# Weight sums of a split product moved from the attention stage to the up product, with a new order in the linear attention

## The chip, the cores and the metric

The kernel runs on one core of one Trainium2 chip. The metric is device time of one execution, in microseconds (us); the median of the runs shown is used. The engines are TensorE (PE: matmuls and transposes, into PSUM), VectorE (DVE), ScalarE (ACT), GpSimd (POOL) and SyncE (SP). SP issues most loads and stores on the hardware queue q1; POOL issues the transfers that add into memory, and others, on the software queue q0. Both queues are carried by the same 16 DMA engines.

## The reference

One layer of a streaming encoder, on 1024 prompt and 32 sample tokens (1056 columns in all), model width 1024:

```python
h = rms_norm(x, g_pre_mix)
qa, ka, va, ra, alr, qb, kb, vb, ga, gb = split_cols(h @ w_in)
oa, s_gla = gla_branch(qa, ka, va, ra, alr, w_a2, b_a2, g_gla, gla_s0, gla_block)
ob, k_rows, v_rows = attn_fn(qb, kb, vb, rel_bias)
mix = (jax.nn.sigmoid(ga) * (oa @ w_br_a) + jax.nn.sigmoid(gb) * (ob @ w_br_b)) @ w_out
x = x + rms_norm(mix, g_post_mix)
f, conv_new = conv_ffn(rms_norm(x, g_pre_ffn), conv_s0, w_up, conv_w, conv_b, w_down)
x = x + rms_norm(f, g_post_ffn)
gate = jax.nn.sigmoid(rms_norm(x, g_pre_ple) @ w_ple_gate)
x = x + rms_norm(gate * (pe @ w_ple), g_post_ple)
```

`gla_branch` is a gated linear attention (4 heads, blocks of tokens with a carried state), `attn_fn` a softmax attention over a band of 64-frame chunks (8 heads), `conv_ffn` an up product of 2 x 2816 columns, a causal convolution of width 3, gelu, and the down product. All is float32; outputs are the new x, the newest band rows, the states of the linear attention and of the convolution.

## The kernel before

Every matrix product is made from split operands: a float32 value is written as a high part and the remainder, and PE makes three products of the parts (high by high, high by low, low by high). The large products save a further eighth by the Strassen-Winograd scheme: an operand is cut into four quarters, sums of quarters are formed, and seven products of sums replace eight. So besides its own weights a product needs *sums of weight quarters*.

The program is one long function, `emit`, with stages one after the other: the per-layer embedding product; the input projection (`in_strassen`); the band attention; the linear attention; the branch products; the out product; the up product (`up_strassen`, 22 blocks f); the down product (28 units of seven by four); the last gate.

**Weight sums.** For the down product they lie in the DRAM tensor `d_ws` (4 sums of 4 parts, 704 KB each), for the branch product in `d_wa` (16 parts of 256 KB). POOL makes each by three DMAs: a one-element write into the target from a tile that has just been computed (`at`; it sets the earliest time), a copy of the first quarter from DRAM to DRAM, and an accumulating copy of the second quarter. The accumulation is put off: `second_sum` keeps a list `later` and issues the oldest entry when more than two are waiting. The down product loads `d_ws[1]` for its fifth unit first.

**Band attention.** For each of four head pairs, two heads: nine steps (j = 0 to 8) of scores, exponentials, transposes and value products; a head is a group g. Engine orders of PE, DVE and ACT follow the program text here; POOL's and SP's are set by a planner. The loop makes one part of a weight sum of `d_wa` at j = 1, 4, 7 and of `d_ws` at j = 2, 5, 8, from the second group on, until there are 16. In the last group the first gate decays of the linear attention are begun (`decays(0)`): POOL loads `d_alr` into a tile that the scores of the group before have used, and the next step's matmul (L1188) reads it. `band_end` turns the sums of the exponentials into reciprocals and stores them to `d_inv` from a tile of tag `ot` (two buffers), which the evacuations L1055 use too.

**Filler.** PE's gaps in both attention stages are filled with pieces of the rest of the input projection: `piece` emits some 9 to 12 matmuls; `fill["n"]` counts pieces. Their PSUM tiles are evacuated by functions kept in `fill["done"]`, called by `flush` (all) or `tidy` (all but the newest). The first 117 pieces belong to plain tiles of three pieces a unit, the next 112 are whole units (`MAIN` = 229). The band runs up to 120 pieces, the preamble of the linear attention up to 126 (`GLA_FIRST`).

**Linear attention.** 16 units u (4 heads by 4 segments). In each: products of the levels into PSUM, score copies by DVE, a transpose of scores (`score_turn`, with ACT's copy into `turned`), the column copy `score_last` by DVE into `turned` (L1453), factors, exponentials and differences for unit u + 1, results of unit u - 1, the outputs (L1521) which read `turned`, the next unit's start, and the inverse roots (`roots`). Nine calls of `slot` a unit may each emit one piece; a condition paces them.

**Up product.** Block f computes one tile of a and one of g. `q` is the single tile of tag `c22` that holds a partial sum (L2586); `av` has three buffers; `sm` (L2367) is a single tile of quarter sums, stored by POOL (L2364). Blocks in `AHEAD` have two of their products made earlier and take 5, not 7. In this loop the planner orders all engines.

Of the kernel before, what the change touches and what calls it, by code (L numbers as in the profile page):

```python
# [114 lines left out]
def emit(tc, a):  # L115
# [118 lines left out]
    def log_exp():  # L234
        tc.keep_in_program_order(ac.preload_act_table_set("natural_log_exp_and_others"))
# [664 lines left out]
    def piece():  # L900
        if fill["now"] is None:
            if fill["at"] == len(units):
                return
            fill["now"] = unit_parts(*units[fill["at"]]), 0
        tidy()
        lows()
        parts, n = fill["now"]
        next(parts)
        i, c = units[fill["at"]]
        item = isinstance(tiles[i], Item)  # L910
        fill["now"] = (parts, n + 1) if n < 2 and not item else None
        if n == 0 and fill["split"] == i + 1 <= FIRST and (c in (0, 2) if item else c < 2):
            split_half(int(c > 0))
            if c:
                fill["lows"].append(load_tile)
        if fill["now"] is None:
            fill["at"] += 1
        fill["n"] += 1
        if fill["n"] in PLACES:
            place(*PLACES[fill["n"]])  # L920

    def flush():
        for f in fill["done"]:
            f()
        fill["done"].clear()
# [226 lines left out]
    def weight_sum(i, m, at):  # L1152
        x, y = WSUMS[i]
        po.dma_start(d_ws[i, m, 0:1, 0:1], at)
        po.dma_start(d_ws[i, m], x[m])
        second_sum(d_ws[i, m], y[m])
# [100 lines left out]
    for i in range(len(WORK) + SK + 1):  # L1257
        g, j = divmod(i, NW)
        hp, hd = divmod(g, 2)
        if g < 8:  # L1260
            if j == 0:
                if hd == 0:
                    band_sums(hp)
                steps = prepare(g + 1) if g < 7 else decays(0)
            if j == 3 and hd == 0:
                B[hp]["ob"] = evt()
            WORK[i][0]()
            if SK <= i:
                WORK[i - SK][1]()
            B[hp]["exp"].pop()()  # L1270
            next(steps, None)
            if j % 3 == 2:
                next(made, None)
            if j % 3 == 2 and g:
                n = 3 * (g - 1) + j // 3
                if n < 16:
                    weight_sum(*divmod(n, 4), B[hp]["sums"][hd][0:1, 0:1])
            if hd == 0 and hp < 3 and j in (5, 7) or hd and hp < 3 and j == 0:
                band_row(hp + 1, {5: 0, 7: 1, 0: 2}[j])
            if g == 7 and j in (6, 7):  # L1280
                head_value(0, j - 6)
            if j % 3 == 1 and g:
                n = 3 * (g - 1) + j // 3
                if n < 4 * HK:
                    branch_sum(n, B[hp]["sums"][hd][0:1, 0:1])
        piece()
        n = i - SK - 1
        if n >= 0 and WORK[n][2]:
            WORK[n][2]()
        if len(WORK) <= i < len(WORK) + SK:  # L1290
            WORK[i - SK][1]()
        for f in LOWS:
            f()
        LOWS.clear()
        flush()
        if fill["n"] < 18 + (BAND_PIECES - 18) * (i + 1) / (len(WORK) + SK + 1):
            piece()
        next(end, None)
        if n >= 0 and n % (2 * NW) == 2 * NW - 1:
            end = band_end(n // (2 * NW))  # L1300
            next(end)
    flush()
    while fill["now"]:
        piece()
        flush()
    next(end)
    while later:
        second_sum()
# [41 lines left out]
    def differences(u, ls):  # L1350
        g, h, s, t0, nt = seg(u)
        b = g["b"]
        if ls[0] == 1:
            X[u] = tl(gp, [P, 8, 288], tag="x", bufs=2)
        x = X[u]
        for l in ls:
            m, w = 1 << l, level_width(l, nt)
            bv = b[:, 0, t0 : t0 + w]
            at, ref = [bass.AP(bv.tensor, bv.offset + o, [bv.ap[0], [2 * m, w // (2 * m)], [T + e, 2], [d, m]]) for o, e, d in ((0, m, 1), (m - 1, 0, 0))]
            ve.tensor_tensor(x[:, l - 1, :w].rearrange("p (n h m) -> p n h m", h=2, m=m), at, ref, op=ALU.subtract)  # L1360
# [91 lines left out]
    def score_last(u):  # L1452
        ve.copy_predicated(turned.rearrange("p (n s) -> p n s", s=2)[:, :, 1], masks[:, 0, 1], R[u]["dg"][:, 0:64])  # L1453
# [198 lines left out]

    slots = [0]

    def slot(k=1):
        for i in range(k):
            slots[0] += 1
            if OB.get("h") is not None or fill["n"] < min(MAIN, GLA_FIRST + (MAIN - GLA_FIRST) * slots[0] / (9 * 14.7)):
                piece()

    level_start(0)
    for u in range(16):
        h, s = divmod(u, 4)
        if s == 0:
            if h == 3:
                rows_times = branch_rows()
                next(rows_times, None)
            if h < 3:
                if h:
                    head(h + 1)  # L1670
                chain = decays(h + 1)
        flush()
        loads(u)
        if u < 15:
            differences(u + 1, range(1, 5))
        if s == 3:
            next(chain, None)

        def states():
            if u < 15:  # L1680
                slot(2)
                key_copies(u)
            if u:
                output_copies(u - 1)
            if u == 15:
                gate_sigmoid(0)
                gate_sigmoid(1)
            if s == 3:
                next(chain, None)
            updates(u)  # L1690

        def turn_back():
            if u == 15:
                slot(2)
            if u:
                output_turns(u - 1)
            slot(1)

        level_products(u, (states, turn_back))
        flush()  # L1700
        if u < 15:
            exponentials(u + 1, (1, 2, 3, 4))
            flush()
        score_copies(u, range(4, 7))
        slot(1)
        score_turn(u)
        if u < 15:
            exponentials(u + 1, (7, 6))
        if u:
            results(u - 1)  # L1710
        if u == 15:
            gates(u)
            gate_sigmoid(2)
            gate_sigmoid(3)
            branch_split(1)
        if u < 15:
            differences(u + 1, (5,))
        score_last(u)
        if u < 15:
            factors(u + 1, (7, 1, 2))  # L1720
        flush()
        slot(1)
        if s == 3:
            next(chain, None)
        if u < 15:
            factors(u + 1, (3, 4, 6))
            exponentials(u + 1, (5,))
        tidy()
        slot()
        flush()  # L1730
        if s < 2 and h:
            turn_values(h, 2 + 4 * s)
        outputs(u)
        if u < 15:
            level_start(u + 1)
        squares_a(u)
        if u < 15:
            factors(u + 1, (5,))
        else:
            branch_split(2)  # L1740
        if u >= 12:
            next(rows_times, None)
        flush()
        n = (5, 4, 2, 0)[s]
        steps_of(lambda: next(chain, None), n - n // 2)
        tidy()
        slot()
        if s < 2 and h:
            turn_values(h, 4 + 4 * s)
        flush()  # L1750
        steps_of(lambda: next(chain, None), n // 2)
        slot()
        if s == 2 and h < 3:
            head_value(h + 1, 0)
            head_value(h + 1, 1)
        if u == 14:
            while fill["n"] < MAIN:
                piece()
                flush()
            xp.release()  # L1760
            key_copies(15)
            eb = pool("eb", side="right")
            bo = pool("bo", side="right")
            for x in "hl":
                OB[x] = tl(bo, [P, 4, T], F32R, tag="b" + x)
            branch_split(0)
            split_tile()
            load_tile()
            gate_rows(1)
        if u == 15:  # L1770
            log_exp()
        roots(u)
        flush()
        if u < 15:
            gates(u)
        if u < 14:
            slot()
        if u == 13:
            next(rows_times, None)
            gate_rows(0)  # L1780
# [713 lines left out]
    def up_strassen(f):  # L2494
# [89 lines left out]
        Z_ = Z[:, :, :HC]  # L2584
        mul(Z, weight(s1, WL_ENG[2]), "t1", True, True)
        ve.tensor_tensor(q, p1, Z_, op=ALU.add)  # L2586
        if not ahead:
            mul(X, weight(a12, WL_ENG[3]), "b21", False, True)
            ac.activation(c11, X_, AF.Copy)
# [704 lines left out]
```

## Time and profile before

| | us |
|---|---|
| median of 3 runs | 1894.21 (1894.15 to 1895.33) |
| profiled execution, its own time | 1898.3 |
| its span, first to last instruction | 1896.4 |
| PE busy in it | 1831.3 |
| granted TensorE clock, mean | 0.988 |

A row of the busy table gives an engine's busy time and its count of instructions. A row of a stretch gives its bounds and length, then the busy time and count for PE, PEld (weight loads), DVE, ACT and POOL, the granted TensorE clock, the busy share of the DMA engines and the GB/s. In a timeline row the first two numbers are start and duration; the bracket at the end is the idle time just before it on that engine, and what ended it. A row of DMA issues gives how many, the KB of one, and the median time from issue to landing. A queue's row gives packets, MB and the share of the 16 engines' time. "waits" rows say who waited for what: total, times, longest.

### The profile page before, as it was taken

How to read it: one execution, taken by the hardware profiler on the slowest of the kernel's cores; microseconds unless marked ns; L12 is line 12 of the kernel's file. 1: busy time of each engine (PE TensorE's matmuls, PEld its weight loads, DVE VectorE, ACT ScalarE, POOL GpSimd, SP SyncE). 2: the span in 40 equal slices, each digit the busy share in tenths (PEclk: the TensorE clock that was granted, in tenths of full speed). 3: DMA queues.
4: the chain of work that ended last, by engine and by line, in shares of the span. 5: the costliest groups of instructions: out<-in, count | busy, mean ns of one | idle time of the engine just before them, and what ended most of it. 6: DMA issues, size and time to landing. Idle time of an engine off the chain costs nothing.

```text
span 1896.4 us, 36233 instructions
## 1 busy us (share of the span) xinstructions
PE 1831.3 (97%) x14000; PEld 1791.7 (94%) x14000; DVE 1301.3 (69%) x2451; ACT 1005.1 (53%) x2126; POOL 369.0 (19%) x641
## 2 busy tenths in 40 slices
PE   8999999999959999999999999999999999999996
PEld 8999998999958999898999999999999999999996
DVE  6955543666625777677856775888888875558776
ACT  7544233666626776766646455433333345555555
POOL 0043431243311222110000111111122210000112
PEclk9999999999979999999999999999999999999998
DMA  7288987799985889976777377455557679887746
GB/s 283 81 232 236 277 205 219 213 257 301 263 199 183 247 240 258 243 172 199 274 221 226 111 267 286 154 196 166 181 168 184 168 202 297 281 292 240 237 150 109
DMA packets 169402, 413.24 MB, mean 218 GB/s; under 512 B 21957, under 2 KB 56973, under 8 KB 168333
## 3 DMA queue, kind: packets, MB, share of 16 engines
q1 hardware_dynamic: 111548, 244.34, 39.5%
q0 software_dynamic: 56240, 161.90, 33.0%
q10 hardware_dynamic: 1440, 4.69, 0.6%
q8 instruction: 110, 1.80, 0.4%
q14 instruction: 64, 0.52, 0.1%
HBM read 270.68 MB, written 181.97 MB: 239 GB/s over the span
## 4 chain that ended last, share of the span: by engine, by line
PE 56%; DVE 4%; ACT 4%; DMA 3%; issue 1%; SPq 1%; DVEq 0%; ACTq 0%; POOLq 0%
PE two L2523 6%; PE two L2521 6%; PE two L2522 6%; PE mm L228 3%; PE mm L226 3%; PE mm L227 3%; PE two L2968 3%; PE two L2966 3%; PE two L2967 3%; PE mm L859 2%; PE mm L860 2%; PE mm L861 2%; PE two L2430 1%; PE two L2432 1%; PE two L2431 1%
## 5 line engine op out<-in xcount | busy, mean ns | idle before, releaser
L2968 PE MATMUL two<-d,wlo 128*128 128x264 f32 x616 | 174.4, 283 | 1.0 <-DVE wlo L2702 1.0
L2967 PE MATMUL two<-d,whi 128*128 128x264 f32 x616 | 174.7, 284 | 0.2 <-DVE d L2653 0.2
L2966 PE MATMUL two<-d,whi 128*128 128x264 f32 x616 | 174.6, 284 | 0.0
L2511 ACT ACTIVATE whi<-ws 128x512 fp32r<-128x512 f32 x88 | 55.5, 632 | 161.5 <-PE two L2522 159.6
L859 PE MATMUL mm<-xh,whi 128*128 128x264 f32 x448 | 134.8, 301 | 3.7 <-ACT fv L867 3.6
L860 PE MATMUL mm<-xl,whi 128*128 128x264 f32 x448 | 127.4, 284 | 0.0
L861 PE MATMUL mm<-xh,wlo 128*128 128x264 f32 x448 | 127.2, 284 | 0.0
L2522 PE MATMUL two<-ml,whi 128*128 128x264 f32 x448 | 126.4, 283 | 0.0
L2523 PE MATMUL two<-mh,wlo 128*128 128x264 f32 x448 | 126.0, 284 | 0.0
L2521 PE MATMUL two<-mh,whi 128*128 128x264 f32 x448 | 125.8, 284 | 0.0
L2968 PEld LDWEIGHTS two<-d,wlo 128*128 128x128 f32 x616 | 116.4, 189 | 1.5 <-DVE wlo L2702 1.5
L2967 PEld LDWEIGHTS two<-d,whi 128*128 128x128 f32 x616 | 115.8, 188 | 0.4 <-DVE d L2653 0.4
L2966 PEld LDWEIGHTS two<-d,whi 128*128 128x128 f32 x616 | 115.7, 188 | 0.0
L890 PE MATMUL mm<-xh,whi 128*128 128x352 f32 x312 | 111.0, 356 | 2.0 <-ACT fv L734 2.0
L892 PE MATMUL mm<-xh,wlo 128*128 128x352 f32 x312 | 103.0, 330 | 0.0
L891 PE MATMUL mm<-xl,whi 128*128 128x352 f32 x312 | 102.8, 330 | 0.0
L642 PE MATMUL two<-tl,whi 128*128 128x264 f32 x320 | 90.7, 284 | 0.0
L641 PE MATMUL two<-th,whi 128*128 128x264 f32 x320 | 90.7, 283 | 0.0
L643 PE MATMUL two<-th,wlo 128*128 128x264 f32 x320 | 90.7, 284 | 0.0
L859 PEld LDWEIGHTS mm<-xh,whi 128*128 128x128 f32 x448 | 84.9, 190 | 5.6 <-ACT fv L867 5.0
L2702 DVE TENSOR_TENSOR wlo<-wraw,whi 128x512 fp32r<-128x512 f32 (+1 forms) x81 | 51.8, 644 | 50.1 <-ACT whi L2701 50.0
L860 PEld LDWEIGHTS mm<-xl,whi 128*128 128x128 f32 x448 | 84.5, 189 | 0.0
(801 smaller groups left out, 6876.7 us busy)
## 6 DMA issues: line engine op xcount, KB each, us to landing
raw<-in_w_in SPq DMA_DIRECT2D x36, 512.0 KB, 6.1
d_b<-av POOLq DMA_DIRECT2D x33, 528.0 KB, 3.3
d_ws<-in_w_down POOLq DMA_DIRECT2D x24, 704.0 KB, 15.0
uraw<-d_b SPq DMA_DIRECT2D x32, 528.0 KB, 5.7
raw<-in_w_up SPq DMA_DIRECT2D x29, 512.0 KB, 4.4
d_gs<-in_w_in POOLq DMA_DIRECT2D x48, 256.0 KB, 5.8
sraw<-in_w_up SPq DMA_DIRECT2D x22, 512.0 KB, 3.6
wraw<-d_ws SPq DMA_DIRECT2D x16, 704.0 KB, 5.8
```

The source lines that it names most:

```text
L859: pe.matmul(ps, h[:, k], xh[:, b, s], start=(k == 0 and not (half and x.chain)), stop=False, skip_group_check=True)
L860: pe.matmul(ps, h[:, k], xl[:, b, s], start=False, stop=False, skip_group_check=True)
L861: pe.matmul(ps, l[:, k], xh[:, b, s], start=False, stop=(k == HK - 1), skip_group_check=True)
L890: pe.matmul(ps, wh, h[:, k, s], start=(k == 0), stop=False)
L891: pe.matmul(ps, wh, l[:, k, s], start=False, stop=False)
L892: pe.matmul(ps, wl, h[:, k, s], start=False, stop=(k == cnt - 1))
L2521: pe.matmul(ps[:, j, :HC], w[0][:, k], x[0][:, k, s], start=st, stop=False, skip_group_check=True)
L2522: pe.matmul(ps[:, j, :HC], w[0][:, k], x[1][:, k, s], start=False, stop=False, skip_group_check=True)
L2523: pe.matmul(ps[:, j, :HC], w[1][:, k], x[0][:, k, s], start=False, stop=sp_, skip_group_check=True)
L2966: pe.matmul(o, wh, xh_[:, s], start=(k == 0 and p in (0, 4, 5)), stop=False, skip_group_check=True)
L2967: pe.matmul(o, wh, xl_[:, s], start=False, stop=False, skip_group_check=True)
L2968: pe.matmul(o, wl, xh_[:, s], start=False, stop=(k == HD - 1 and p in (3, 4, 6)), skip_group_check=True)
```

## The change

The 16 sums of `d_ws` are no longer made in the band; block f of the up product makes part f (for f below 16), held back by its tile `q`, and blocks 16 and 17 issue the last two accumulations. At the band's end exactly one more piece runs, where the kernel before ran pieces until the current unit was done. In the linear attention the pacing of the pieces becomes a fixed pattern: of nine slots the fifth and eighth are left out. The column copy `score_last` goes ahead of the results of unit u - 1 and of the splits and sigmoids of the last unit, and behind the differences of level 5 and the factors of levels 1 and 2, which now come earlier; one `flush` is added between the exponentials of levels 7 and 6; the factors of level 7 come last. In unit 14 the roots are made before the branch operands are split.

```diff
-            if j % 3 == 2 and g:
-                n = 3 * (g - 1) + j // 3
-                if n < 16:
-                    weight_sum(*divmod(n, 4), B[hp]["sums"][hd][0:1, 0:1])
...
     flush()
-    while fill["now"]:
-        piece()
-        flush()
+    piece()
+    flush()
     next(end)
...
+    SKIP = (5, 8)
+
     def slot(k=1):
         for i in range(k):
             slots[0] += 1
-            if OB.get("h") is not None or fill["n"] < min(MAIN, GLA_FIRST + (MAIN - GLA_FIRST) * slots[0] / (9 * 14.7)):
+            if OB.get("h") is not None or fill["n"] < MAIN and slots[0] % 9 not in SKIP:
                 piece()
...
         score_turn(u)
         if u < 15:
-            exponentials(u + 1, (7, 6))
+            exponentials(u + 1, (7,))
+            flush()
+            exponentials(u + 1, (6,))
+            differences(u + 1, (5,))
+            factors(u + 1, (1, 2))
+        score_last(u)
         if u:
             results(u - 1)
...
         if u < 15:
-            differences(u + 1, (5,))
-        score_last(u)
-        if u < 15:
-            factors(u + 1, (7, 1, 2))
+            factors(u + 1, (7,))
         flush()
...
+        if u == 15:
+            log_exp()
+        roots(u)
+        if u == 14:
             branch_split(0)
             split_tile()
             load_tile()
             gate_rows(1)
-        if u == 15:
-            log_exp()
-        roots(u)
...
         ve.tensor_tensor(q, p1, Z_, op=ALU.add)
+        if f < 16:
+            weight_sum(*divmod(f, 4), q[0:1, 0, 0:1])
+        elif f < 18:
+            second_sum()
```

## The prediction

> **What bounds the kernel now.** I read the page's busy table first, then the stretches by stage, then the waits of TensorE, and only then the timeline around the longest of them.
>
> ```profile
> PE 1831.3 (97%) x14000; PEld 1791.7 (94%) x14000; DVE 1301.3 (69%) x2451; ACT 1005.1 (53%) x2126; POOL 369.0 (19%) x641
> ```
> ```profile
> 340.00:520.00 180.00, 177.22 (x1239) 170.00 (x1238) 113.08 (x282) 119.60 (x290) 61.29 (x123) 1.00 0.95 259
> 520.00:545.00 25.00, 19.45 (x127) 18.35 (x126) 10.20 (x24) 10.34 (x27) 3.28 (x8) 0.86 1.03 252
> 545.00:565.00 20.00, 5.29 (x26) 5.02 (x25) 1.14 (x5) 2.26 (x6) 3.53 (x6) 0.66 0.67 158
> 600.00:890.00 290.00, 281.15 (x2060) 261.86 (x2059) 215.94 (x615) 212.78 (x718) 62.44 (x91) 0.99 0.85 235
> 1205.00:1560.00 355.00, 355.00 (x2928) 355.00 (x2927) 300.53 (x489) 136.13 (x183) 69.80 (x132) 1.00 0.61 176
> ```
>
> TensorE (PE, the first busy column) bounds the program: it idles 65 us of 1896.4. So an edit is worth the idle time and lost clock of PE that it removes. The rows are, from the top, the band attention (two parts), its end, the linear attention and the up product. The up product has no idle PE to win, but the last two columns show DMA engines only 61% busy; the band runs them at 95 to 103%. The linear attention idles 8.9 us. The remarkable place is 520 to 565: PE works 24.7 us out of 45.
>
> ```profile
> 523.40 0.82 POOL L1138 DMA_DIRECT2D d_wa<-sums  x1
> 544.71 0.56 POOL L1139 DMA_DIRECT2D d_wa<-in_w_br_a  x1 [19.59 <-DMA d_wa<-sums]
> 549.77 0.83 POOL L1132 DMA_DIRECT2D d_wa<-in_w_br_a  x1 [4.01 <-DMA d_wa<-in_w_br_a]
> 551.27 0.84 POOL L1132 DMA_DIRECT2D d_ws<-in_w_down  x1 [0.66 <-DMA d_ws<-d_ws]
> 551.80 0.86 POOL L1183 DMA_DIRECT2D qs<-d_alr  x1
> ```
> ```profile
> 514.48 0.30 SPq L1175 DMA_DIRECT2D d_inv<-ot  x1
> ...
> 536.64 0.38 ACT L1055 ACTIVATE ot<-one 64x256 f32<-64x256 f32 x1 [6.65 <-DMA d_inv<-ot]
> ...
> 531.55 0.29 PE L1036 MATMUL two<-kl,qs 128*32 128x272 f32 x1
> 538.76 0.47 PE L1035 MATMUL two<-kh,qs 128*128 128x128 f32 x1 [5.30 <-DVE sm L1041]
> 561.76 0.63 PE L1188 MATMUL one<-qs,wa 80*128 80x352 f32 x1 [14.71 <-DMA qs<-d_alr]
> ```
>
> There are two stalls. **The 5.30 us stall:** ACT's evacuation L1055 needs the tile that the 9 KB store of the reciprocal sums still reads, and that store, issued at 514.48, held ACT until 536.64; DVE waits for ACT, PE for DVE. **The 14.71 us stall:** the gate matmul L1188 needs d_alr, whose load POOL issued only at 551.80, because POOL stood 19.59 us on a one-element write and then queued the last sums ahead of the load. Both are DMA delays, and the traffic is on record:
>
> ```profile
> qs<-d_alr POOLq DMA_DIRECT2D x1, 330.0 KB, 9.8
> ```
> ```profile
> q0 software_dynamic: 8032, 30.48, 64.5%
> ...
> d_ws<-in_w_down POOLq DMA_DIRECT2D x23, 704.0 KB, 15.1
> d_wa<-in_w_br_a POOLq DMA_DIRECT2D x24, 256.0 KB, 13.1
> ```
> ```profile
> L1154 POOL DMA_DIRECT2D d_ws<-sums x16: 497/511/817, 351.2 to 523.9; - x16
> ...
> DMA to landing us min/median/max: 4.5/7.5/8.6
> ```
>
> (DMA issues, first from 520 to 562, then queues and issues from 351 to 551, then from the answers on the tiles d_ws and d_inv, with ns min/median/max and first and last start.) POOL's queue q0 takes two thirds of what the engines have. Over the 200 us its 30.48 MB cost 129 us of all 16 engines, 4.23 us a MB. The d_ws sums are 16 copies and 16 accumulations of 704 KB (0.721 MB), so 98 us; the same 32 of 256 KB for d_wa (36 us) stay.
>
> **A. Weight sums leave the band.** 98 us of engine time leave some 200 us (351 to 551), so the busy share falls from about 0.95 to about 0.5. POOL loses 48 issues, the 16 one-element writes with their landing waits among them. The d_inv store then meets half the traffic: ACT wanted its tile at 529.99 (536.64 - 6.65), 15.5 us after the issue, and the other transfers of d_inv land in 4.5 to 8.6 us. I take 5.30 us as gone; at the 22 us of this one it would stay.
>
> ```profile
> d_b<-av POOLq DMA_DIRECT2D x33, 528.0 KB, 3.3
> ```
>
> For the d_alr load the cover is the PE work between the last reader of the old tile (531.55) and L1188: 1.6 us to the first stall (533.46), then 8.3 us to 547.05, of which 2.8 is half clock; 7.1 us. Its need is 0.86 issue plus a landing between 3.3 us (POOL's larger store above) and 9.8 (this one, behind two accumulations): 4.2 to 10.7, so 0 to 3.6 us stay. Nearest is the lower end, since one accumulation of 256 KB at most is ahead; I keep 1.0.
>
> The clock goes with the stalls:
>
> ```profile
> 535.00:540.00 5.00, 0.99 (x5) 0.81 (x6) 2.83 (x8) 2.44 (x6) 0.00 (x0) 0.76 1.08 255
> 540.00:545.00 5.00, 5.00 (x26) 4.91 (x25) 0.00 (x0) 0.84 (x4) 0.29 (x1) 0.56 1.02 332
> ...
> 560.00:565.00 5.00, 3.24 (x12) 3.20 (x12) 0.00 (x0) 1.00 (x2) 0.00 (x0) 0.50 0.26 54
> 565.00:570.00 5.00, 5.00 (x23) 4.71 (x24) 2.08 (x7) 3.17 (x9) 0.00 (x0) 0.67 0.10 36
> ```
>
> Half clock covers 1.2 + 4.4 us of PE work after the first stall and 3.2 + 3.3 after the second; half of that, 2.8 and 3.3 us, is lost. The Trainium skill (TensorE: Matmul & The Clock Gate, What's actually happening) says that an idle window of some 3.4 us halves the clock and a busy one restores it. The trace agrees that the clock halves after both stalls, but it stays half longer than one such window; by the rule alone each stall would cost 1.7 us of clock, 3.4 in place of 6.1, and the forecast would be 2.7 us later.
>
> A gives 5.3 + 14.7 + 2.8 + 3.3 - 1.0 = **25.1 us**.
>
> **B. The same sums in the up product.** Per block f = 0 to 15: a one-element write after the sum L2586, a copy, and the accumulation of two blocks earlier; POOL issues 0.5 + 0.5 + 0.8 us and has 285 idle us there. PE, DVE and ACT get no instruction. The copy waits on POOL for the landing of the one-element write, as the gate sums of the input projection do:
>
> ```profile
> d_gs<-c POOLq DMA_DIRECT2D x32, 0.0 KB, 3.8
> ```
>
> Behind it stand POOL's memsets of gx, which it issues ahead, and the stores of av and sm, for which DVE waits only when their tiles come round. The DMA engines get 98 us over 18 of 22 blocks (0.82 of 355 us, 290), so 0.61 becomes 0.95. What is late then? Two tiles are tight (timeline, DMA issues, timeline):
>
> ```profile
> 1228.10 0.70 DVE L2367 TENSOR_TENSOR sm<-av 128x528 f32<-128x528 f32 x1
> 1241.90 0.70 DVE L2367 TENSOR_TENSOR sm<-av 128x528 f32<-128x528 f32 x1
> ...
> 1229.10 0.77 POOL L2364 DMA_DIRECT2D d_b<-sm  x1 [0.25 <-DVE sm L2367]
> ```
> ```profile
> d_b<-sm POOLq DMA_DIRECT2D x11, 792.0 KB, 6.8
> ...
> sraw<-in_w_up SPq DMA_DIRECT2D x22, 512.0 KB, 3.6
> ```
> ```profile
> 1429.11 0.33 SPq L2497 DMA_DIRECT2D sraw<-in_w_up  x1
> ...
> 1436.57 0.69 DVE L2504 TENSOR_TENSOR ws<-sraw 128x512 f32<-128x512 f32 x1
> ```
>
> The tile sm is single and written every 13.8 us; its store is issued by 1229.87 and lands 6.8 us later, 8.6 us after the write began, so 5.2 us are spare. A copy and an accumulation ahead of it in q0 cost 98 / 16 = 6.1 us: 0.9 us late, and DVE, busy 300.5 of 355 us, has 2.1 spare per 13.8. The second weight tile has 7.5 us from issue to use and lands in 3.6. So cost is between nothing and the rivals below; as TensorE runs with several products of split weights in hand, I take **2 us**, near the lower end. An earlier stage gives the same pattern (one-element writes, copies and accumulations behind q) at 82% of DMA with PE at 201.47 of 202:
>
> ```profile
> 85.00:287.00 202.00, 201.47 (x1658) 201.47 (x1659) 107.08 (x161) 78.05 (x113) 79.47 (x127) 1.00 0.82 231
> ```
>
> The sums are first read by the down product, well after block 17.
>
> **C. One more piece at the band's end** (12 matmuls, already in the work) fills the wait for the reciprocals, but the preamble of the linear attention loses it:
>
> ```profile
> 597.57 0.38 PE L1172 MATMUL one<-ident,sums 128*9 128x128 f32 x2 [1.19 <-DVE sums L1167]
> ```
>
> Between -1.2 and +1.2 us, the wait gone or moved there; I take 0.
>
> **D. The linear attention's order.** No instruction is added; the waits are PE's 8.9 us. The old condition, counted out from 126 pieces, skips slots 5 and 1 of every unit's nine; the new one skips 5 and 8, the same seven pieces a unit, so one piece moves from before the roots to the next unit's state update. PE's waits there, 590 to 905 (us in total, times, longest), and the last unit's:
>
> ```profile
> PE mm L859 <- ACT fv L867: 3.6, 6, 1.4
> ```
> ```profile
> 883.97 0.67 PE L1521 MATMUL one<-vt,turned 128*128 128x256 f32 x2 [1.31 <-DVE turned L1453]
> ```
>
> In the last unit the column copy (L1453) stood behind a result and four splits; it now goes before them, so 1.3 us go. The extra flush brings evacuations forward (L859), the extra early piece needs one more bank evacuated behind ACT's key and output copies. Up to the stage's whole 8.9 us may go; up to one evacuation a unit may come (0.38 us for 256 columns in the L1055 row, 6 us for 16); I take **-1.3**.
>
> **Sum.** -25.1 + 2 + 0 - 1.3 = -24.4 us. The profiled execution took 1898.3 us around its span of 1896.4; the median of the runs shown is 1894.2, 0.2% less; I take the stalls to be the same in both. So 1873.9 profiled, **1870 us** for the runs.
>
> **Rivals.**
> 1. *The sum tile becomes the wait (slower).* If q0 shares the engines with SP's loads packet by packet, the 6.1 us become 12.2: sm lands 7.0 us late, 4.9 beyond DVE's spare, in the 13 shorter blocks (those in AHEAD) that carry sums: +64 us, about 1932. It decides from a delay of 9.2 us in q0 (5.2 spare + 2.1 + 24.4/13). For it: DMA at 0.95 and single sm. Against: the earlier stage. Chance 0.08. The Trainium skill (DMA: Bandwidth & Descriptors, Queues, rings and completion order) has the engines alternate between queues packet by packet, which is this rival's premise; the 22 us of a 9 KB store agree.
> 2. *The same in part*, a delay of 8 to 9 us: +10, 1880. Chance 0.14.
> 3. *d_alr stays late*: 3.6 us plus a half-clock stretch of 3.3: 1876. Chance 0.08.
> 4. *The moved filler waits for banks*: +6 and no gain in D: 1877. Chance 0.10.
> 5. *The band doesn't notice*: the remaining d_wa and SP traffic keeps the stalls, 1893. Against: 98 of 134 us of the sums go. Chance 0.03.
>
> **The numbers.** The forecast has 0.57. A change within 0.2% (3.8 us) can't be told from none. Faster: forecast, rivals 2 to 4: 0.89. Same: rival 5 and a weak form of 1, 0.04. Slower 0.07. The range runs from 1861 (no cost in B, and most of D's waits gone: 1894.2 - 26.1 - 7) to 1885 (rivals 2 and 4 with little to spare), leaving rivals 1 and 5 and combinations out.
>
> **What would show it.** Right: no wait on d_inv or d_alr above 2 us at the band's end, full clock from 520 to 590, DMA share near 0.5 there and 0.9 in the up product with PE still 100% busy. B is wrong if DVE's L2367 waits for d_b<-sm or L2504 for sraw and PE idles between 1180 and 1540; D is wrong if L859 waits for ACT in most units. The prediction falls if PE's two stalls are still there under lighter DMA.

## The result, and the profile after

| | before | after |
|---|---|---|
| median of the runs, us | 1894.8 (1894.15 to 1897.75, 4 runs) | 1882.3 (1877.64 to 1885.08, 4 runs) |
| ratio, 95% interval | | 0.9929 [0.9906, 0.9952] |
| profiled execution and its span, us | 1898.3, 1896.4 | 1877.64, 1875.9 |

The changed kernel is faster by 12.5 us, about half of the 24.4 us forecast; the time lies inside the range. The profiled execution is the fastest of its four, 4.7 us under their median.

To place the difference, the span is cut where TensorE first runs a matmul of the next stage. These are the rows of the answers on single lines (line, engine, operation, tiles, count; ns min/median/max, first and last start); the L1035 row holds the band's score matmuls, the up product's first matmul is in the t2h row, the down product's in the d row:

```profile
L1035 PE MATMUL two<-kh,qs x112: 222/308/689, 316.4 to 586.3; 128*128 128x320 f32 x64, 128*32 128x272 f32 x16, 128*128 128x128 f32 x8, 128*128 128x256 f32 x8
...
L2521 PE MATMUL two<-t2h,whi x176: 281/285/289, 1201.5 to 1551.0; 128*128 128x264 f32 x176
...
L2966 PE MATMUL two<-d,whi x616: 281/283/337, 1557.2 to 1784.3; 128*128 128x264 f32 x154
```
```profile
L1035 PE MATMUL two<-kh,qs x112: 222/309/477, 311.7 to 556.7; 128*128 128x320 f32 x64, 128*32 128x272 f32 x16, 128*128 128x128 f32 x8, 128*128 128x256 f32 x8
...
L2521 PE MATMUL two<-t2h,whi x176: 281/285/289, 1168.2 to 1531.4; 128*128 128x264 f32 x176
...
L2970 PE MATMUL two<-d,whi x616: 281/283/339, 1537.6 to 1764.3; 128*128 128x264 f32 x154
```

The upper three are of before, the lower three of after. The up product took 1557.2 - 1201.5 = 355.7 us and takes 369.4. The band, from the first to the last start of its score matmuls, took 269.9 and takes 245.0. So **the band gave 24.9 us and the up product took 13.7 of it back**. From there to the up product it was 615.2 and is 611.5; from the down product's start to the end, 339.2 and 338.3. The remaining 4.7 us lie ahead of the band (316.4 against 311.7), where nothing was changed; that start lay between 311.7 and 317.4 us in the profiled executions of this study, and is not counted as an effect.

The windows after, in the same columns as before the change (us, busy time and count of each engine, granted clock, DMA share, GB/s):

```profile
520.00:545.00 25.00, 24.46 (x168) 23.59 (x168) 12.68 (x37) 15.90 (x43) 1.07 (x2) 1.00 0.37 114
545.00:565.00 20.00, 19.22 (x144) 18.55 (x143) 12.30 (x31) 13.46 (x31) 0.83 (x2) 1.00 0.31 109
...
1205.00:1560.00 355.00, 346.05 (x2814) 345.50 (x2813) 287.18 (x464) 135.01 (x184) 97.28 (x171) 0.99 0.84 235
```

At the band's end both stalls are gone, the clock is full, and the DMA share is 0.31 to 0.37. The load of d_alr, which TensorE had waited for, lands in 3.7 us (DMA issues, 520 to 562):

```profile
qs<-d_alr POOLq DMA_DIRECT2D x1, 330.0 KB, 3.7
```

In the up product TensorE now idles. The waits from 1180 to 1545 (engine, tile and line, what it waited for: us in total, times, longest), and one stretch in order of time:

```profile
POOL d_ws L1155 <- DMA d_ws<-c: 74.4, 13, 7.6
POOL d_ws L1132 <- DMA d_ws<-in_w_down: 26.3, 7, 5.4
POOL d_ws L1132 <- DMA d_ws<-d_ws: 23.1, 6, 5.5
DVE ws L2504 <- DMA sraw<-in_w_up: 22.5, 11, 5.4
DVE sm L2367 <- DMA d_b<-sm: 10.6, 4, 4.4
...
PE two L2521 <- DVE av L2580: 9.0, 3, 4.7
```
```profile
1387.72 0.70 DVE L2367 TENSOR_TENSOR sm<-av 128x528 f32<-128x528 f32 x1
...
1392.57 0.54 POOL L1155 DMA_DIRECT2D d_ws<-d_ws  x1 [5.36 <-DMA d_ws<-c]
...
1393.09 2.05 POOL L2364 DMA_DIRECT2D d_b<-av  x2
...
1394.84 3.00 POOL L2364 DMA_DIRECT2D d_b<-sm  x1
```
```profile
1404.90 0.33 SPq L2582 DMA_DIRECT2D av<-d_e  x1
1405.32 0.38 SPq L2497 DMA_DIRECT2D sraw<-in_w_up  x1
...
1406.26 0.71 DVE L2367 TENSOR_TENSOR sm<-av 128x528 f32<-128x528 f32 x1 [4.19 <-DMA d_b<-sm]
...
1411.60 0.69 DVE L2504 TENSOR_TENSOR ws<-sraw 128x512 f32<-128x512 f32 x1 [2.81 <-DMA sraw<-in_w_up]
```

Read the stretch from the top. GpSimd's copy stands 5.36 us for the landing of the one-element write. The stores of av and sm are behind it in GpSimd's order, so sm, written from 1387.72 on, is sent off only from 1394.84. SyncE's load of av (L2582), which may not overwrite the tile before its store has landed, starts at 1404.90, and the next weight load, sraw, directly behind it in SyncE's order. VectorE then waits 4.19 us for sm's store and 2.81 for sraw; TensorE stands for 3.40 us at 1414.99. SyncE's own waits on that store (the same view for SyncE's queue) were and are:

```profile
SPq L2582 <- DMA d_b<-av: 3.3, 3, 1.6
```
```profile
SPq L2582 <- DMA d_b<-av: 46.7, 8, 11.3
```

The clock adds to TensorE's 9.0 us of idle time:

```profile
1400.00:1440.00 40.00, 36.60 (x282) 36.42 (x281) 28.09 (x48) 12.79 (x18) 16.75 (x25) 0.91 0.92 228
1440.00:1480.00 40.00, 35.25 (x278) 35.08 (x278) 30.27 (x52) 11.64 (x16) 6.73 (x14) 0.96 0.72 193
```

36.60 x 0.09 + 35.25 x 0.04 = 4.7 us of work are lost to the reduced clock behind the two longer stalls (3.40 and 4.75 us), and 9.0 + 4.7 is the whole 13.7 us.

### The profile page after: what moved, and what is told of

Its sections match the earlier page's. It is cut to its first block, busy times and chain, and to the rows that moved or that the text cites. A ratio compares the mean times of both kernels' runs of the same rounds, so it can differ in the third digit from the quotient of the medians.

```text
span 1875.9 us, 36253 instructions
## 1 busy us (share of the span) xinstructions
PE 1828.2 (97%) x14000; PEld 1790.9 (95%) x14000; DVE 1298.5 (69%) x2451; ACT 1004.4 (54%) x2126; POOL 370.7 (20%) x641
## 4 chain that ended last, share of the span: by engine, by line
PE 78%; DMA 6%; DVE 6%; ACT 5%; issue 4%; POOL 1%; SPq 0%; DVEq 0%; ACTq 0%; POOLq 0%
PE two L2521 5%; PE two L2523 5%; PE two L2522 5%; PE two L641 4%; PE two L642 4%; PE two L643 4%; PE two L2970 3%; PE mm L228 3%; PE mm L226 3%; PE two L2972 3%; PE two L2971 3%; PE mm L227 3%; PE mm L890 3%; PE mm L892 2%; PE mm L891 2%
## 5 line engine op out<-in xcount | busy, mean ns | idle before, releaser
L859 PE MATMUL mm<-xh,whi 128*128 128x264 f32 x448 | 135.2, 302 | 3.6 <-ACT fv L867 3.5
L890 PE MATMUL mm<-xh,whi 128*128 128x352 f32 x312 | 108.6, 348 | 1.0 <-ACT fv L734 1.0
L859 PEld LDWEIGHTS mm<-xh,whi 128*128 128x128 f32 x448 | 85.0, 190 | 5.5 <-ACT fv L867 4.9
```

The source lines that it names most:

```text
L859: pe.matmul(ps, h[:, k], xh[:, b, s], start=(k == 0 and not (half and x.chain)), stop=False, skip_group_check=True)
L890: pe.matmul(ps, wh, h[:, k, s], start=(k == 0), stop=False)
```

## The experiments

Three theories of the loss were put against each other. **ORDER**: GpSimd's in-order waits for landings hold the stores. **LOAD**: the DMA engines are simply too busy (share 0.61 before, 0.84 after). **The sum tile**: sm, of which there is one, becomes the wait. All times below are medians; "up" is the length of the up product as above, in the one profiled execution of the run. The kernel before took 1896.8, 1897.8, 1897.0 and 1894.3 us beside the runs a, b, c and d.

| run | time, us | ratio to before, 95% | up, us | SyncE's wait on av's store, us |
|---|---|---|---|---|
| changed kernel | 1882.3 | 0.9929 [0.9906, 0.9952] | 369.4 | 46.7 |
| a1 no sums | 1867.6 | 0.9853 [0.9828, 0.9878] | 355.7 | |
| a2 sums back in the band | 1892.6 | 0.9986 [0.9971, 1.0000] | 355.7 | |
| a3 copy meant one block later | 1885.6 | 0.9939 [0.9918, 0.9961] | 375.0 | 53.9 |
| a4 two tiles sm | 1883.4 | 0.9931 [0.9905, 0.9956] | 375.0 | 52.7 |
| b1 write and copy behind c21 | 1911.0 | 1.0069 [1.0043, 1.0095] | 403.4 | 121.3 |
| b2 waits without traffic | 1867.2 | 0.9836 [0.9818, 0.9855] | 355.6 | 5.9 |
| b3 12 in the band, 4 in the up product | 1866.7 | 0.9836 [0.9818, 0.9855] | 357.1 | 14.2 |
| b4 all in the band, a group earlier | 1880.5 | 0.9907 [0.9889, 0.9925] | 355.6 | |
| c1 no one-element write | 1864.8 | 0.9846 [0.9809, 0.9882] | 355.7 | 6.9 |
| c2 accumulations gated too | 1873.3 | 0.9891 [0.9858, 0.9924] | 366.5 | 20.5 |
| c3 copy behind the stores | 1869.3 | 0.9869 [0.9840, 0.9898] | 357.4 | 30.0 |
| d1 SyncE's order | 1875.3 | 0.9886 [0.9845, 0.9927] | 365.7 | 11.4 |

### What each part is worth: a1 and a2

a1 drops the call in the up product and has the down product load plain quarters; a2 drops it and puts the old call back into the band:

```diff
-        if f < 16:
-            weight_sum(*divmod(f, 4), q[0:1, 0, 0:1])
-        elif f < 18:
-            second_sum()
```
```diff
+            if j % 3 == 2 and g:
+                n = 3 * (g - 1) + j // 3
+                if n < 16:
+                    weight_sum(*divmod(n, 4), B[hp]["sums"][hd][0:1, 0:1])
```

> The changed kernel without any weight sums of the down product (the sums are left out, and the down product loads plain quarters of w_down, of the same size, in their place). If the sums are what the up product lost by (355 us before, 369.4 us in the changed kernel), it takes 355 to 357 us again, with no PE idle time there, and the median is 1861 to 1866, some 18 us below the changed kernel's 1882. If the loss comes from the planner's new order in the up product, the time stays above 1875.

> The changed kernel with the weight sums back in the band: only the last piece of the band and the new order of the linear attention are left of the change. If the prediction's split holds, both stalls at the band's end are back and these parts alone are worth 1 to 4 us: 1890 to 1894. If a part of the 33 us won before the up product is theirs, it is below 1888.

Without sums the up product is back at 355.7 us, so the whole loss there is the sums' doing. With the sums back in the band both stalls are back (waits, 340 to 600):

```profile
PE one L1188 <- DMA qs<-d_alr: 15.6, 1, 15.6
...
PE two L1035 <- DVE sm L1041: 5.7, 3, 4.2
```

So the band's 24.9 us are the sums leaving it. What a2 keeps, the new order of the linear attention and the extra piece, is worth 1896.8 x (1 - 0.9986) = 2.7 us, with an interval from nothing to 5.5.

### The sum tile, and a first try at the order: a4 and a3

```diff
-tl(sw, [P, HT], tag="sm", bufs=1)
+tl(sw, [P, HT], tag="sm", bufs=2)
```

> The changed kernel with two tiles sm in place of one. Theory sm (the single tile is what DVE is late by): DVE no longer waits for d_b<-sm (10.6 us in 4 waits), PE idles less than 4 us in the up product, median 1869 to 1875. Theory order: the sraw waits (22.5 us in 11) stay, as they come from SP's queue, and the median is 1877 to 1882. Theory load: as theory order.

> The changed kernel; in the up product each copy is issued one block after its one-element write, so that POOL no longer waits for that write's landing (74 us in 13 waits). The traffic is the same. Theory order (POOL's wait holds the stores of av and sm behind it, the late av holds SP's av load and the sraw load behind that): the landing wait is below 10 us, PE idles less than 3 us in the up product, median 1866 to 1871. Theory load (the DMA engines are too busy): PE still idles 8 us or more there, median 1878 to 1883.

With a second tile (a4) the waits on sm disappear and the time stays: the wait on sraw takes their place (37.1 us against 22.5), with up to 9.2 us at a time.

```profile
POOL d_ws L1155 <- DMA d_ws<-c: 101.0, 16, 10.1
...
DVE ws L2504 <- DMA sraw<-in_w_up: 37.1, 12, 9.2
...
PE two L2521 <- DVE av L2580: 12.8, 5, 6.6
```

So the sum tile alone isn't the cause. a3 missed its aim: the copy was written into the code one block later, but GpSimd's order, which the planner makes here, put it right behind the one-element write again, and GpSimd waited 91.9 us for these writes. It tells the theories apart in nothing; c3 repeats it with the order pinned.

### A later issue, and waits without traffic: b1 and b2

b1 makes the call behind the c21 addition, with an element of gx as the source; b2 moves one row of 128 in each copy and accumulation.

```diff
+        ve.tensor_tensor(c21, p1, Y_, op=ALU.add)
+        if f < 16:
+            weight_sum(*divmod(f, 4), gx[0:1, 2:3])
```
```diff
-        po.dma_start(d_ws[i, m], x[m])
-        second_sum(d_ws[i, m], y[m])
+        po.dma_start(d_ws[i, m, 0:1], x[m][0:1])
+        second_sum(d_ws[i, m, 0:1], y[m][0:1])
```

> The sixteen copies and accumulations stay in the up product, with all their traffic, but the one-element write that starts each copy is made behind the block's c21 addition, so that GpSimd's queue issues the stores of av and of sm first and waits for the write's landing after them. Theory ORDER (GpSimd's wait of 74.4 us in 13 holds the stores, SyncE's load of av waits for the stores and holds the load of sraw behind it): the up product goes back from 369.4 (fastest execution) and 375.0 to 355 to 359 us, and the time to 1867 to 1872. Theory LOAD (the DMA engines, busy to 0.84 with 98 us of added traffic, land sraw, sm and av late whatever the order): the up product stays at 367 to 375 and the time at 1878 to 1886.

> Each copy and accumulation in the up product moves one row of 128 only; the rest of the sums is left out, and the down product loads plain quarters in their place. GpSimd's one-element writes, its waits and its issues stay, the traffic goes. LOAD: the up product is back at 355.7 us as without sums, the time at 1866 to 1870. ORDER in its pure form (the wait costs whatever the traffic is): the up product keeps at least 8 of its 13.7 to 19 us, the time stays at 1876 or above. If the one-element write lands late only because the engines are full (both together), this run looks as LOAD says while the run with the later issue looks as ORDER says.

b1 came out against both theories as they were put: the up product is 34 us longer than in the changed kernel, 47.7 longer than without sums, and the kernel is slower than before. Yet in the up product the instructions of TensorE, VectorE, ScalarE and SyncE stand in the same order (so they do in a1, c1, c2 and c3), the bytes are the same, and the DMA share of the window is lower, 0.79 against 0.84. What differs is GpSimd:

```profile
POOL d_ws L1155 <- DMA d_ws<-gx: 142.2, 16, 11.7
DVE sm L2367 <- DMA d_b<-sm: 67.8, 15, 7.3
```
```profile
1384.50 1.15 POOL L1154 DMA_DIRECT2D d_ws<-gx  x1
1394.19 0.57 POOL L1155 DMA_DIRECT2D d_ws<-in_w_down  x1 [8.53 <-DMA d_ws<-gx]
...
1399.91 0.86 POOL L1132 DMA_DIRECT2D d_ws<-in_w_down  x1 [4.76 <-DMA raw<-in_w_up]
1400.46 2.31 POOL L2364 DMA_DIRECT2D d_b<-av  x2
1401.96 1.75 POOL L2364 DMA_DIRECT2D d_b<-sm  x1
```

Now the write stands in q0 behind the block's own stores and lands later still; GpSimd waits 8.53 us for it, then 4.76 ahead of the accumulation, and the *next* block's stores come after both. So ORDER was right that GpSimd's waits decide, and my arrangement of them was wrong. b2, where the rest of each sum is left out and the down product loads plain quarters, shows that the waits without the traffic are harmless: the one-element writes land in 2.8 us in place of 6.3, GpSimd stands 31.7 us for them in place of 74.4, and nothing is lost. In b2 half of LOAD and half of ORDER fit; c1 was made to part them.

```profile
d_ws<-c POOLq DMA_DIRECT2D x16, 0.0 KB, 6.3
```
```profile
d_ws<-c POOLq DMA_DIRECT2D x16, 0.0 KB, 2.8
```

(DMA issues from 1168 to 1530, of after and of b2.)

### The sums in other places: b3 and b4

```diff
+                if n < 12:
+                    weight_sum(*divmod(n, 4), B[hp]["sums"][hd][0:1, 0:1])
...
-        if f < 16:
-            weight_sum(*divmod(f, 4), q[0:1, 0, 0:1])
+        if f < 4:
+            weight_sum(3, f, q[0:1, 0, 0:1])
```
```diff
+            if j % 3 == 2:
+                n = 3 * g + j // 3
+                if n < 16:
```

> The first twelve sums are made in the band as in the kernel before, the last four (quarter 3) in the up product's blocks 0 to 3. If the band's two waits (15.6 us for qs<-d_alr, 4.2 for ot) come from the last sums' traffic at the band's end, they go as in the changed kernel; four sums cost the up product 0 to 5 us at what sixteen cost (13.7 to 19, a quarter of it, or nothing as the first blocks have spare). Expected: band to recurrence 246 to 250 us, up product 355.7 to 360, time 1867 to 1873. If the band's waits come from the sums of the whole band: 1885 to 1893.

> All sixteen sums in the band, each one group earlier than in the kernel before, none in the up product; the linear attention as changed. If only the traffic in the band's last 40 us delays ot and d_alr, the waits shrink to under 4 us in sum and the time is 1867 to 1873 with the up product at 355.7; if they come from the band's whole load, the waits stay near 20 us and the time at 1888 to 1893 as with the sums in their old places.

b3 has twelve sums in the band at a DMA share of 0.96 and loses nothing there: the band is 245.0 us long with twelve sums as with none. Without the last four the 24.9 us are gone. The rows of b3, the band's first part and its end:

```profile
340.00:520.00 180.00, 177.25 (x1242) 169.81 (x1241) 113.10 (x280) 119.32 (x287) 57.65 (x119) 1.00 0.96 260
520.00:545.00 25.00, 24.46 (x170) 23.43 (x170) 12.30 (x36) 15.71 (x42) 2.45 (x4) 1.00 0.55 154
```

b4, one group earlier, is in between: the wait on d_alr shrinks from 15.6 us (a2) to 6.2, more than the 4 us in sum that the expectation allowed, and the band is 261.8 us long. But a good part of that loss is new and lies at the band's other end. Three sums now start together in the first group, three small loads of SyncE (s<-in_w_a, 32 KB each) land 7.1 us after their issue, ScalarE waits 8.7 us for them, and TensorE, behind ScalarE and VectorE, 8.1 us at 331 us (waits from 310 to 340; a2 has 0.5 there). So b4 doesn't show how early the sums would have to end. Whether the last four did their harm by coming late or by being too many isn't told apart either.

```profile
PE one L1188 <- DMA qs<-d_alr: 6.2, 1, 6.2
```

### The wait on a landing taken out or moved: c1, c2 and c3

c1 lets the copy wait for the VectorE addition itself; c2 does the same for the accumulation, two blocks later; c3 keeps the one-element write and pins the copy behind the block's stores.

```diff
-        po.dma_start(d_ws[i, m, 0:1, 0:1], at)
-        po.dma_start(d_ws[i, m], x[m])
+        ins = po.dma_start(d_ws[i, m], x[m])
+        tc.add_manual_dep(ins.ins, at.ins.name, ...)
```
```diff
+        behind(at, po.dma_start(d_ws[i, m], x[m]))
+        later.append((d_ws[i, m], y[m]))
+        if len(later) > 2:
+            behind(at, po.dma_start(*later.pop(0), accum_op=ALU.add))
```
```diff
         activate(f, gx, av)
+        if f < 16:
+            late_copy(*divmod(f, 4))
```

> All sixteen sums in the up product with all their traffic; the one-element write is gone, and the copy waits instead for the same VectorE addition by a semaphore, so that GpSimd has no landing to wait for ahead of its stores (the accumulations still wait for the landings of their copies). ORDER, as the run with the later issue left it (GpSimd's in-order waits for landings that the traffic has made long, and not the traffic alone): the 74.4 us of waits on d_ws<-c go, GpSimd keeps the 49 us behind the accumulations; the up product 357 to 365 us, the time 1868 to 1877. LOAD (the DMA engines' share alone): up product 369 to 375, time 1880 to 1886.

> As the run without the one-element write, and each accumulation also waits for the VectorE addition of two blocks later, where its copy has landed long ago: the same traffic, and no landing of the sums that GpSimd still waits for. ORDER: the up product 355.7 to 359 us, the time 1866 to 1871. LOAD: up product 369 to 375, time 1880 to 1886. In between (360 to 368): both have a share, and the difference to the run before is what the accumulations' waits cost.

> The one-element write stays where the changed kernel makes it, and the copy is held in GpSimd's order behind the block's stores of av and sm, so that the write has some 7 us to land before GpSimd waits for it: what the run with the deferred copy was meant to test. ORDER: the wait on d_ws<-c falls from 74.4 to under 30 us, the up product to 356 to 364, the time to 1867 to 1876. LOAD: up product 369 to 375, time 1880 to 1886.

c1 settles the question of the load. All of the copies and accumulations are there, the engines are busier than in the changed kernel (0.87, 249 GB/s), sraw still lands in 7.3 us and sm in 10.3 to 10.5, and TensorE never idles in the up product:

```profile
1205.00:1560.00 355.00, 355.00 (x2929) 355.00 (x2928) 292.58 (x466) 141.91 (x194) 90.89 (x152) 1.00 0.87 249
```
```profile
SPq L2582 <- DMA d_b<-av: 6.9, 3, 3.7
```
```profile
sraw<-in_w_up SPq DMA_DIRECT2D x20, 512.0 KB, 7.3
```

LOAD in its plain form has fallen: the same traffic, moved in less time, costs nothing here. Not all of GpSimd's waits are gone, though. c1 still has those ahead of the accumulations:

```profile
POOL d_ws L1132 <- DMA d_ws<-in_w_down: 18.4, 6, 4.1
POOL d_ws L1132 <- DMA d_ws<-d_ws: 18.1, 7, 5.6
```

c3, at a share of 0.89 and with the write kept, has even 62.1 + 52.1 = 114.2 us of them, hardly less than the 123.8 us of landing waits in the changed kernel; they stand behind the block's stores, and the up product takes 357.4 us. So it is not the sum of these waits that costs; what differs is that the changed kernel has 74.4 us of them right ahead of the stores of av. c2 did not do what ORDER expected. No landing of the sums is waited for any more, and yet the interval of its ratio overlaps that of the changed kernel (0.9858 to 0.9924 and 0.9906 to 0.9952), and the profiled execution (the slowest of its four; the others took 1870 to 1875) lost 10.8 us in the up product. In it the copy and the accumulation go out together, right ahead of the stores of av:

```profile
1408.93 0.55 POOL L1157 DMA_DIRECT2D d_ws<-d_ws  x1 [0.54 <-DVE c L2590]
1409.48 0.89 POOL L1160 DMA_DIRECT2D d_ws<-in_w_down  x1
1410.88 2.00 POOL L2368 DMA_DIRECT2D d_b<-av  x2 [0.51 <-DVE av L2363]
```

In the stretch from 1385 to 1425 the stores of av landed 12.2 us after their issue in the median, SyncE's load of av waited 6.6 us for one of them with the load of sraw behind it, and VectorE then stood 7.26 us for sraw. So a store is late either because GpSimd can't issue it, or because two large transfers stand ahead of it in q0; c1 has the same two further apart in the block, with the stores of av between them. That it is this pair in c2 is read from one execution and wasn't tested by itself.

### Which path from the late store to TensorE: d1

d1 is the changed kernel with one difference: on SyncE the load of av is issued behind the next block's load of sraw.

```diff
+        if av_load:
+            tc.add_manual_dep(av_load.pop().ins, ld.ins.name, ...)
...
-            dma.dma_start(c11, v2(d_e[AHEAD.index(f), :, one]))
+            av_load.append(dma.dma_start(c11, v2(d_e[AHEAD.index(f), :, one])))
```

> Everything as in the changed kernel, GpSimd's order and its waits on the one-element writes included; on SyncE's queue alone the load of av (L2582), which waits for the store of av, is issued behind the next block's load of sraw instead of ahead of it. If the loss in the up product comes through SyncE (the load of av waits 46.7 us in sum for d_b<-av, and sraw's load stands behind it): DVE's wait on sraw falls from 22.5 to under 8 us, the up product to 355.7 to 360 us, the time to 1866 to 1872. If it comes through the sum tile sm (DVE's 10.6 us on d_b<-sm, which this leaves) or through av itself: up product 365 to 372, time 1876 to 1883. If av, loaded later, becomes the wait itself: DVE waits on av<-d_e, up product above 369.

It falls between the two. The time, 1875.3, has an interval that overlaps that of the changed kernel (0.9845 to 0.9927 and 0.9906 to 0.9952), so its gain of some 7 us isn't sure. The waits show what stays:

```profile
POOL d_ws L1155 <- DMA d_ws<-c: 88.2, 14, 10.4
DVE sm L2367 <- DMA d_b<-sm: 21.7, 8, 3.3
...
DVE ws L2508 <- DMA sraw<-in_w_up: 12.2, 8, 4.0
...
PE two L2525 <- DVE av L2584: 4.7, 2, 3.5
```

The wait on sraw falls from 22.5 to 12.2 us, the wait on sm doubles to 21.7. There are two paths from a held store to VectorE, by the tile sm and by SyncE's queue to sraw; with either one cleared (a4, d1) the other takes over part or all. In the profiled executions, taking GpSimd's wait away from ahead of the stores did more than clearing one path: the up product took 355.7 (c1) and 357.4 us (c3), against 375.0 (a4) and 365.7 (d1).

## Why the prediction came out as it did

**A, the band: right in kind and size.** Forecast 25.1 us, found 24.9. Both stalls and both half-clock stretches went. The 1.0 us kept for d_alr was not needed: it landed in 3.7 us, near the lower end of the 3.3 to 9.8 that the prediction had. Rivals 3 and 5 are out. One thing the prediction didn't see: it took 98 us of traffic spread over the stage as what delays the end, and b3 shows that twelve of sixteen sums could have stayed.

**B, the up product: the mechanism half seen, the size wrong.** Forecast 2 us, found 13.7 in the fastest execution, and 12.5 us of gain in all where 24.4 were forecast. This is the whole error. Two places of the step failed:

- "The copy waits on POOL for the landing of the one-element write", taken as 3.8 us from the input projection. It landed in 6.3 us in the median, and GpSimd stood 74.4 us for it, 49.4 more for the copies ahead of the accumulations. The row of the earlier stage, which was to show that the pattern is harmless at a share of 0.82, could not show it: GpSimd has stores behind the copies there too (d_t), but no engine of that stage waits for one of them to land, and the wait on the writes is 12.1 us in all.
- "Behind it stand [...] the stores of av and sm, for which DVE waits only when their tiles come round." The step listed what stands behind GpSimd's wait, but not who else waits for those stores: SyncE's load of av does, and the load of sraw stands behind that. The 7.5 us "from issue to use" of sraw were counted from an issue that itself came some 7.5 us late: in the stretch above it stands 22.6 us behind the issue before it, in a1 at the same place 15.1. What the step did price, a longer stay of sm's store in q0, was the smaller part: that store (792 KB) landed in 8.7 us where it took 6.8, but in the stretch above it was issued 7.1 us after sm was begun, where the row of before has 1.0.

What the prediction said would show B wrong, waits at L2367 and L2504 with TensorE idle, is what the waits after show. Rival 1's share of the engines between queues was not the mechanism, nor was the sum tile alone: a4 took it away without a gain, and c1 ran the same bytes at 0.87 without a loss. Rival 2, "the same in part", gave 1880 and so nearly the time found, but for a delay in q0 at sm, which is one of two paths; that its number came so close, and that the range made room for the time, is in part luck.

**C and D: right within what can be told.** Forecast -1.3 us together, found -2.7 (0 to -5.5) in a2. The wait of 1.31 us in the last unit is gone from the trace, and L859's waits for ScalarE stayed as they were (3.6 us before, 3.5 after), so rival 4 is out. More than that can't be told here: from the last score matmul to the branch product's first matmul (L890, mm<-bh) it took 284.6 us before and 280.3 to 286.6 in the thirteen profiled executions with the new order.

**The version to take.** c1, the changed kernel with the one-element write replaced by a wait on the addition, gives 1864.8 us and TensorE fully busy in the up product. b3, which splits the sums twelve to four, gives 1866.7. Both lie beside the 1867.6 of the kernel without any weight sums (a1): the cost of the sums is gone in either, and which of the two is better can't be told (intervals 0.9809 to 0.9882 and 0.9818 to 0.9855).

## What to carry to other kernels

When a transfer is moved into another stage, write down for its in-order queue not only what is issued behind its wait, but who waits for each of those, through the other queues, down to the compute engine. Don't use the landing of a small transfer as a clock on a busy queue: its landing grows with the traffic that it is meant to time, and a semaphore of the engine that produces the value does the same without it. And a DMA share near 0.9 said nothing by itself here (nothing was lost at 0.87 in c1, nor at 0.96 in the band of b3): look for the single load or store that has less time than it takes to land, at the stage's end above all.

## What the runs showed that was not expected

- The same sums cost the up product nothing, 13.7 us or 47.7 us, by GpSimd's order and waits alone, and the cheapest had the second highest DMA share of all (0.87; 0.84 and 0.79 in the others, 0.89 in c3).
- A one-element write on q0 landed in 2.8 us without the sums' traffic, 6.3 with it and 10.3 where it stood behind the block's stores (b1):

```profile
d_ws<-gx POOLq DMA_DIRECT2D x16, 0.0 KB, 10.3
```

- Idle times of 3.40 and 4.75 us on TensorE cost another 4.7 us by the granted clock. The first lost more than the second, though it was shorter (windows of after):

```profile
1415.00:1420.00 5.00, 5.00 (x23) 5.00 (x24) 4.72 (x6) 1.90 (x4) 1.87 (x4) 0.50 1.05 223
...
1457.00:1462.00 5.00, 4.63 (x25) 4.66 (x26) 4.61 (x8) 1.09 (x1) 0.31 (x3) 0.66 0.36 105
```

The Trainium skill (TensorE: Matmul & The Clock Gate, What's actually happening) has the clock restored after at least one busy window of about 3.4 us; by an estimate from that figure, one such window at half clock loses 1.7 us of work. The second stall agrees with one window (4.63 x 0.34 = 1.6 us); behind the first, twice as much was lost (36.60 x 0.09 = 3.3 us).
